# Rows of the down products' moving operand 64 bytes longer, in a gated encoder layer on one core

## The chip, the cores and the metric

The kernel runs on one core of a Trainium2 chip. A core has five engines that run side by side: TensorE (PE; its weight loads have a row of their own, PEld), VectorE (DVE), ScalarE (ACT), GpSimd (POOL) and SyncE (SP), which here only starts DMA transfers. Data for the engines lie in SBUF, a memory of 128 partitions; products of TensorE land in PSUM. The metric is the device time of one execution in microseconds (us). Before the change it is 1501.67 us, the median of three runs (1501.54 to 1502.61).

## The reference, cut to what matters

One layer of an encoder over 256 tokens with 2048 features, all in 32-bit floats. First come a normalization, an input projection, two kinds of attention with gates, and an output projection. Then, and this is the part that the change touches, a gated MLP with 5632 inner features:

```python
hf = rms_norm(x, ffn_norm[i])
g = dwconv_centred(hf @ w_ffn_gate[i], conv_w[i], conv_b[i])
x = x + (jax.nn.gelu(g) * (hf @ w_ffn_up[i])) @ w_ffn_down[i]
gate_p = jax.nn.sigmoid(rms_norm(x, ple_norm[i]) @ w_ple_gate[i])
x = x + gate_p * (p[i] @ w_ple_proj[i])
return rms_norm(x, final_norm)
```

The product with `w_ffn_down` is called the down product here.

## The kernel before, in words

Features lie on the partitions and tokens along the rows, so a product of a 128x128 weight block with 128 features of all 256 tokens is one step. To keep the precision of 32-bit floats on TensorE's float32r path, each operand is split into a high part and a remainder. A row of a moving operand (the one that streams through TensorE) holds the high parts of 256 tokens and then their remainders, 2T = 512 numbers or 2048 bytes.

*The weights.* All weights come as one stream of 128x128 blocks, in the order of use, by DMA from SyncE into `raw` (L174, three buffers of 16 blocks). For every eight blocks ACT makes the high parts `whi` (L190) and DVE the remainders `wlo` (L191), four buffers each. A block is 512 bytes of a partition.

*A step.* `block` (L195) multiplies the high block with the whole row (L201, 512 columns) and the remainder block with the row's first half (L202, 256 columns). Both add into a PSUM tile `acc`, of which three are used in turn. `product` (L207) runs the steps of one output block one after another; `wide_product` (L214) is the other way about, with weights streaming, for the attention values and the last two projections.

*The order.* `_plan` writes a list of jobs by hand, and the loop at L672 carries them out: the input projection with attention among it (`q`, `k`, `v`), gates and branch products (`ga`, `gb`, `ba`, `bb`), output projection (`o`), then twice, once for each half of the inner features: 22 gate (`g`) and 22 up (`u`) products of 16 steps each, and 16 down products (`d0`, `d1`) of 22 steps each. The small projection of the embedding (`pp`) and its gate (`pg`) come last. Work that follows a product is issued right behind it by `after` (L522) or at a step of a later job by `at`. Each engine works off its own instructions in the order of issue and waits on semaphores for the others.

*The moving operands.* `hs` (input projection and gates), `merged` (output projection) and `hf` (gate and up products) are tiles of the pool `big`, all named `mov` in the profile; `yab` holds the attention's results for the branch products. The down products read `act`, 22 rows, from the pool `ff`, allocated once for each half (L682) in one buffer. The last lines of `after` for an up product fill a row of it: `halves` copies the high part on ACT (L263) and subtracts on DVE (L264). Row k of `act` meets weight block k of the job.

*Places.* The allocator puts `act` at byte 154112 of each partition, behind it in the same pool `c`, `gw` (gate path), `pr`, `pw` (the embedding, `pw` split for the small projection), `ss`, `half`, `gate` and `sq4`. `mov` tiles are at 76960 and 109728, `whi` from 44192 and `wlo` from 60576.

Of the kernel before, what the change touches and what calls it, by code (L numbers as in the profile page):

```python
# [11 lines left out]
FR = mybir.dt.float32r  # L12
# [4 lines left out]
P = 128  # L17
T = 256
# [14 lines left out]
FHALF = FC // 2  # L33
# [100 lines left out]
def _encoder(ctx: ExitStack, tc, xt, pt, cols, table, onehot, mask, ident_in, last_gain, wts, out):  # L134
# [72 lines left out]
    def product(i, moving, n):  # L207
        acc = ps.tile([P, 2 * T], F32, name="acc", bufs=3)
        for k in range(n):
            run_due(i, k)  # L210
            block(acc, moving(k), k == 0, k == n - 1)
        return acc

    def wide_product(i, still, n, w, tag, places=HALVES, late=0):  # L214

        accs = [ps.tile([P, W4], F32, name="acc", tag=tag, bufs=3 if tag == "acc" else 2) for _ in places]

        def step(k, t, hi, lo):
            xh, xl = (still[:, k, c:c + T][:, places[t]] for c in (0, T))
            acc = accs[t][:, :w * P]
            nc.tensor.matmul(acc, xh, hi, start=(k == 0), stop=False)  # L224
            nc.tensor.matmul(acc, xh, lo, start=False, stop=False)  # L225
            nc.tensor.matmul(acc, xl, hi, start=False, stop=(k == n - 1))  # L226

        later = []
        for k in range(n):
            run_due(i, k)  # L230
            b = state["at"]
            s, o = _SUB_OF[b]
            split_to(s + 3)
            hi, lo = (m[:, o:o + w, :] for m in subs[s])
            step(k, 0, hi, lo)
            if k < n - late:
                step(k, 1, hi, lo)
            else:
                later.append((k, 1, hi, lo))
            state["at"] = b + w  # L240
            if o == _SUBS[s] - w:
                del subs[s]
        return accs, lambda: [step(*a) for a in later]
# [5 lines left out]
    def gather(acc, scale=1.0, u=None, keep=lambda ins: ins):  # L249

        t = sc.tile([P, T], F32, name="t")
        keep(nc.scalar.activation(t, acc[:, T:], AF.Copy, scale=scale))  # L252
        if u is None:
            u = sc.tile([P, T], F32, name="u")
        if scale == 1.0:
            nc.vector.tensor_tensor(u, acc[:, :T], t, op=ALU.add)  # L256
        else:
            nc.vector.scalar_tensor_tensor(u, acc[:, :T], scale, t, op0=ALU.mult, op1=ALU.add)
        return u

    def halves(dst, src):

        nc.scalar.activation(dst[:, :T], src, AF.Copy)  # L263
        nc.vector.tensor_tensor(dst[:, T:], src, dst[:, :T].bitcast(F32), op=ALU.subtract)  # L264
# [15 lines left out]
    def sums(totals, columns):  # L280

        s = ps.tile([P, len(columns)], F32, name="misc")
        for c, tokens in enumerate(columns):
            for i, total in enumerate(totals):
                nc.tensor.matmul(s[:, c:c + 1], total[:, tokens], ones[:, :1], start=(i == 0),
                                 stop=(i == len(totals) - 1))
        return s

    def root(s, n):

        v = sc.tile([P, n], F32, name="rv", bufs=3)
        nc.vector.tensor_scalar(v, s, 1.0 / D, EPS, op0=ALU.mult, op1=ALU.add)
        r = sc.tile([P, n], F32, name="rr", bufs=3)
        nc.gpsimd.tensor_tensor(r, v, mhalf[:, :n], op=ALU.pow)
        return r
# [15 lines left out]
    def rms(i, total, key, columns=HALVES):  # L311

        def ask():
            rc[key], dg = norm([total], columns)

            def tell():
                b = spread(dg)
                rt[key] = sc.tile([P, T], F32, name="rms")
                nc.scalar.activation(rt[key], b, AF.Copy)
            at(i[1], tell)  # L320
        at(i[0], ask)


    due, rt, rc, held = {}, {}, {}, {}

    def at(i, f, *a):

        due.setdefault(i, []).append((f, a))
# [343 lines left out]
    for i, job in enumerate(_JOBS):  # L672
        kind, n, _, _, _, blocks = job
        if kind == "ba" and n == 0:
            held["merged"] = big.tile([P, KC, 2 * T], FR, name="mov")
        if kind == "o" and n == 0:
            att.close()
            ff = held["ff"] = ctx.enter_context(tc.tile_pool(name="ff", bufs=1))
            held["hf"] = big.tile([P, KC, 2 * T], FR, name="mov")
            held["tot"] = sc.tile([P, T], F32, name="tot")  # L680
        if kind == "g" and n % FHALF == 0:
            held["act"] = ff.tile([P, FHALF, 2 * T], FR, name="act")  # L682
        if kind == "d1" and n == 0:
            held["pl"] = big.tile([P, KC, 2 * T], FR, name="mov")
            held["tot"] = sc.tile([P, T], F32, name="tot")
            pr = ff.tile([P, 2, T], F32, name="pr")
            nc.scalar.dma_start(pr, pt)
            pw = ff.tile([P, 2, 2 * T], FR, name="pw")
            for k in range(2):
                halves(pw[:, k, :], pr[:, k, :])  # L690
            held["ps"] = pw
            spare = big.tile([P, 2 * KC * T], F32, name="mov")
            held["rows"] = spare[:, :2 * D].rearrange("p (t n) -> p t n", t=2)
            held["lg"] = spare[:, 2 * D:3 * D]
            nc.scalar.dma_start(held["lg"], last_gain)
            held["ss"] = ff.tile([P, 2, QUARTERS], F32, name="ss")
        if kind == "g" and n == 0:
            rms([(i, 14), (i + 1, 9)], held["tot"], 1)
        if kind == "d1" and n % 2:
            at((i + 1, 9 if n < KC - 1 else 1), flip, n - 1)  # L700
        if kind == "pp" and n == 0:
            held["ph"] = ff.tile([P, 2, QUARTERS, W4], F32, name="ph", tag="act")
        if kind == "pp" and n == 2:
            half = held["half"] = held["ff"].tile([P, 2], F32, name="half")
            nc.vector.tensor_scalar(half, root(sums([held["tot"]], HALVES), 2), 0.5, None, op0=ALU.mult)
        if i < FIRST:
            firsts[i] = gather(firsts[i], SCALE if kind == "q" else 1.0,
                               ap_.tile([P, T], F32, name="first", tag="k", bufs=7), keep)
            continue
        if i == FIRST:  # L710
            rms([(START, 6), (START, 12)], tot, 0, HALVES + TWINS)
            for c, (h0, h) in enumerate([(0, 4), (4, 4), (8, 4), (12, 4), (16, 4)]):
                at(((FIRST, 8), (START + 1, 8), (START + 3, 8), (START + 5, 8), (START + 7, 8))[c], bias, h0, h)
        last = i == len(_JOBS) - 1
        rest = None
        if kind == "v":
            far = n[0] >= KVH + HG
            acc, _ = wide_product(i, hs, blocks, len(n), "sp" if far else "acc", TWINS if far else HALVES)
        elif kind in ("pp", "pg"):
            tag = "sp" if kind == "pp" else ("pt", "acc")[n % 2]  # L720
            acc, rest = wide_product(i, held["ps" if kind == "pp" else "pl"], blocks, 4, tag, late=4 if last else 0)
        else:
            acc = product(i, movers[kind], blocks)
        if i == FIRST:
            for e in range(FIRST):
                late = max(e - KVH, 0)
                at((START + late, 5 if late else 13), after, _JOBS[e], START, None, firsts[e])
            at((START, 13), after, job, START, acc)
        elif kind == "g" and n == 0:
            at((i + 1, 10), after, job, i, acc)  # L730
        elif kind == "pg":
            for t in range(2):
                if t:
                    rest()
                gate(n, t, acc[t], last)
                if last:
                    finish(t)
        else:
            after(job, i, acc)
# [48 lines left out]
```

## Time and profile before

| | |
|---|---|
| median of three runs | 1501.67 us (1501.54 to 1502.61) |
| profiled execution, whole | 1501.95 us |
| its span, first to last instruction | 1500.1 us |
| granted TensorE clock, mean | 0.998 |
| busy: PE, PEld | 1483.0 us, 1292.5 us |
| busy: DVE, ACT, POOL | 1045.0 us, 767.0 us, 4.6 us |
| DMA | 280.92 MB, 187 GB/s on average |
| down products, first half | 894.7 to 1018 us of the span |
| down products, second half | 1261.9 to 1388.6 us of the span |

A row of a group of instructions reads: line, engine, operation, output tile <- input tiles, shape, count, then busy time and mean duration, or least, median and largest duration with the first and the last start. Matmuls overlap: one is listed for longer than it keeps the next one waiting, since their ends are modelled. How fast TensorE goes through its steps is therefore read from starts, not from durations. "128*128 128x512" is a weight block of 128x128 with 512 columns streamed past it. Times within the span are counted from its start.

### The profile page before, as it was taken

How to read it: one execution, taken by the hardware profiler on the slowest of the kernel's cores; microseconds unless marked ns; L12 is line 12 of the kernel's file. 1: busy time of each engine (PE TensorE's matmuls, PEld its weight loads, DVE VectorE, ACT ScalarE, POOL GpSimd, SP SyncE). 2: the span in 40 equal slices, each digit the busy share in tenths (PEclk: the TensorE clock that was granted, in tenths of full speed). 3: DMA queues.
4: the chain of work that ended last, by engine and by line, in shares of the span. 5: the costliest groups of instructions: out<-in, count | busy, mean ns of one | idle time of the engine just before them, and what ended most of it. 6: DMA issues, size and time to landing. Idle time of an engine off the chain costs nothing.

```text
span 1500.1 us, 21525 instructions
## 1 busy us (share of the span) xinstructions
PE 1483.0 (99%) x8392; PEld 1292.5 (86%) x8392; DVE 1045.0 (70%) x1631; ACT 767.0 (51%) x1175; POOL 4.6 (0%) x9
## 2 busy tenths in 40 slices
PE   9999999999999999999999999999999999999996
PEld 8888888888888888888888888888888888888885
DVE  7685764666676776778888885557888887656564
ACT  7564544445555555555555554444555555555553
POOL 0000000000000000000000000000000000000000
PEclk9999999999999999999999999999999999999999
DMA  8744344445555555555555555554555555554552
GB/s 316 254 156 182 137 168 172 169 169 188 181 193 196 182 184 204 177 216 194 182 188 194 196 184 183 195 190 180 192 197 191 182 190 196 177 189 172 193 196 84
DMA packets 45233, 280.92 MB, mean 187 GB/s; under 512 B 4996, under 2 KB 9860, under 8 KB 12876
## 3 DMA queue, kind: packets, MB, share of 16 engines
q1 hardware_dynamic: 44268, 277.31, 51.7%
q10 hardware_dynamic: 864, 2.24, 0.4%
q8 instruction: 66, 1.08, 0.3%
q14 instruction: 35, 0.29, 0.1%
HBM read 277.39 MB, written 2.14 MB: 186 GB/s over the span
## 4 chain that ended last, share of the span: by engine, by line
PE 96%; DVE 2%; DMA 1%; ACT 1%; issue 0%; POOL 0%; SPq 0%; DVEq 0%; POOLq 0%; ACTq 0%
PE acc L201 53%; PE acc L202 27%; PE acc L224 4%; PE acc L226 4%; PE acc L225 4%; PE first L201 1%; PE first L202 1%; DVE wlo L191 1%; DMA raw<-in_wts 1%; PE pt L484 0%; PE misc L633 0%; DMA x<-in_xt 0%; PE misc L499 0%; PE sp L449 0%; ACT whi L190 0%
## 5 line engine op out<-in xcount | busy, mean ns | idle before, releaser
L191 DVE TENSOR_TENSOR wlo<-raw,whi 128x1024 fp32r<-128x1024 f32 (+1 forms) x519 | 632.0, 1218 | 407.4 <-ACT whi L190 407.1
L201 PE MATMUL acc<-mov,whi 128*128 128x512 f32 x2608 | 911.4, 394 | 1.5 <-DVE v L539 1.5
L190 ACT ACTIVATE whi<-raw 128x1024 fp32r<-128x1024 f32 (+1 forms) x519 | 547.6, 1055 | 645.0 <-PE acc L201 394.0
L202 PE MATMUL acc<-mov,wlo 128*128 128x256 f32 x2608 | 728.2, 279 | 0.0
L201 PEld LDWEIGHTS acc<-mov,whi 128*128 128x128 f32 x2608 | 488.6, 187 | 112.0 <-DVE v L539 1.7
L202 PEld LDWEIGHTS acc<-mov,wlo 128*128 128x128 f32 x2608 | 491.9, 189 | 0.2
L201 PE MATMUL acc<-act,whi 128*128 128x512 f32 x704 | 247.5, 394 | 0.0
L202 PE MATMUL acc<-act,wlo 128*128 128x256 f32 x704 | 196.5, 279 | 0.0
L201 PEld LDWEIGHTS acc<-act,whi 128*128 128x128 f32 x704 | 131.9, 187 | 31.1
L202 PEld LDWEIGHTS acc<-act,wlo 128*128 128x128 f32 x704 | 132.0, 187 | 0.0
L224 PE MATMUL acc<-whi,mov 128*128 128x512 f32 (+1 forms) x256 | 96.9, 379 | 0.0
L226 PE MATMUL acc<-whi,mov 128*128 128x512 f32 (+1 forms) x256 | 96.6, 377 | 0.0
L225 PE MATMUL acc<-wlo,mov 128*128 128x512 f32 (+1 forms) x256 | 96.6, 377 | 0.0
L252 ACT ACTIVATE t<-acc 128x256 f32<-128x256 f32 x227 | 83.1, 370 | 23.2 <-PE acc L202 23.2
L256 DVE TENSOR_TENSOR u<-acc,t 128x256 f32<-128x256 f32 x196 | 81.3, 418 | 2.4 <-ACT t L252 2.4
L201 PE MATMUL acc<-yab,whi 128*128 128x512 f32 x192 | 68.4, 395 | 0.0
L224 PEld LDWEIGHTS acc<-whi,mov 128*128 128x128 f32 x256 | 48.6, 190 | 9.3 <-DVE wlo L191 0.8
L226 PEld LDWEIGHTS acc<-whi,mov 128*128 128x128 f32 x256 | 48.6, 190 | 8.8
L225 PEld LDWEIGHTS acc<-wlo,mov 128*128 128x128 f32 x256 | 48.6, 190 | 8.6
L202 PE MATMUL acc<-yab,wlo 128*128 128x256 f32 x192 | 53.8, 280 | 0.0
L201 PEld LDWEIGHTS acc<-yab,whi 128*128 128x128 f32 x192 | 36.0, 188 | 8.8
L201 PE MATMUL first<-mov,whi 128*128 128x512 f32 x112 | 39.0, 400 | 0.8 <-DVE mov L269 0.8
(137 smaller groups left out, 856.5 us busy)
## 6 DMA issues: line engine op xcount, KB each, us to landing
raw<-in_wts SPq DMA_DIRECT2D x251, 1024.0 KB, 4.8
raw<-in_wts SPq DMA_DIRECT2D x12, 512.0 KB, 6.9
x<-in_xt SPq DMA_DIRECT2D x13, 128.0 KB, 6.0
mov<-hold SPq DMA_DIRECT2D x3, 514.0 KB, 6.4
mov<-hold SPq DMA_DIRECT2D x2, 768.0 KB, 7.1
mov<-in_last_gain ACTq DMA_DIRECT2D x1, 1024.0 KB, 4.8
out<-mov SPq DMA_DIRECT2D x2, 384.0 KB, 2.5
out<-mov ACTq DMA_DIRECT2D x2, 384.0 KB
```

What stands on the lines that cost most here:

```text
L190: nc.scalar.activation(hi, src, AF.Copy)
L191: nc.vector.tensor_tensor(lo, src, hi.bitcast(F32), op=ALU.subtract)
L201: nc.tensor.matmul(acc, hi[:, o, :], m, start=first, stop=False, skip_group_check=True)
L202: nc.tensor.matmul(acc[:, T:], lo[:, o, :], m[:, :T], start=False, stop=last, skip_group_check=True)
L224: nc.tensor.matmul(acc, xh, hi, start=(k == 0), stop=False)
L225: nc.tensor.matmul(acc, xh, lo, start=False, stop=False)
L226: nc.tensor.matmul(acc, xl, hi, start=False, stop=(k == n - 1))
L252: keep(nc.scalar.activation(t, acc[:, T:], AF.Copy, scale=scale))
L256: nc.vector.tensor_tensor(u, acc[:, :T], t, op=ALU.add)
```

## The change

Each row of `act` is allocated 16 numbers (64 bytes) longer, and the tile is cut back to its first 512 numbers per row at once, so that everything else reads and writes it as before:

```diff
         if kind == "g" and n % FHALF == 0:
-            held["act"] = ff.tile([P, FHALF, 2 * T], FR, name="act")
+            held["act"] = ff.tile([P, FHALF, 2 * T + 16], FR, name="act")[:, :, :2 * T]
```

Row k then starts at 154112 + 2112k bytes instead of 154112 + 2048k. The weight blocks stay where they are, 512 bytes apart, so the place of a row relative to its weight block, taken modulo 512 bytes, goes on by 64 bytes from each step to the next. The tiles behind `act` in the pool start 22 x 64 = 1408 bytes later.

## The prediction

> **What bounds the kernel now.** I read the page from the top (busy times, then the chain that ended last), then the busy times by stage, then the first and last start of the matmuls that read one operand, which give the spacing of a step.
>
> ```profile
> span 1500.1 us, 21525 instructions
> PE 1483.0 (99%) x8392; PEld 1292.5 (86%) x8392; DVE 1045.0 (70%) x1631; ACT 767.0 (51%) x1175; POOL 4.6 (0%) x9
> PE 96%; DVE 2%; DMA 1%; ACT 1%; issue 0%; POOL 0%; SPq 0%; DVEq 0%; POOLq 0%; ACTq 0%
> L201 PE MATMUL acc<-act,whi 128*128 128x512 f32 x704 | 247.5, 394 | 0.0
> L202 PE MATMUL acc<-act,wlo 128*128 128x256 f32 x704 | 196.5, 279 | 0.0
> ```
>
> TensorE is busy 99% of the span and carries 96% of the chain. The change touches the 704 pairs of matmuls that read `act`: 2 halves of 16 down products with 22 steps each, one L201 (512 columns) and one L202 (256 columns) per step. Neither line waited at all. By stage (stretch; length; busy time per engine; granted clock; DMA share; GB/s), the rows being the whole of the first half's down products, the second half's gate and up products, and the second half's down products:
>
> ```profile
> 894.50:1018.00 123.50, 123.50 (x707) 107.82 (x707) 67.74 (x80) 52.20 (x62) 0.00 (x0) 1.00 0.54 189
> 1018.00:1261.80 243.80, 243.80 (x1408) 214.94 (x1407) 198.65 (x349) 125.22 (x197) 0.00 (x0) 1.00 0.53 190
> 1261.80:1388.60 126.80, 126.80 (x734) 110.64 (x733) 78.37 (x109) 66.68 (x98) 0.00 (x0) 1.00 0.50 183
> ```
>
> In these stages PE is full at clock 1.00, while DVE works 67.74 of 123.50 us, ACT 52.20, and the DMA engines 54%. So the time here is the number of pairs times the spacing of a pair, and only a change of spacing can count.
>
> A matmul's listed duration (394 ns) overlaps the next one's and is no spacing. The spacing comes from the rows of a tile: first and last start, divided by the count less one. In order, for 512-column matmuls: `act` in the first half, `hf` (a tile named mov) in the second half's gate and up products, `merged` (also named mov) in the output projection, `yab` in the last branch products:
>
> ```profile
> L201 PE MATMUL acc<-act,whi x352: 392/394/397, 894.7 to 1017.5; 128*128 128x512 f32 x176
> ...
> L201 PE MATMUL acc<-mov,whi x673: 391/391/391, 1022.7 to 1255.7; 128*128 128x512 f32 x169
> ...
> L201 PE MATMUL acc<-mov,whi x206: 395/398/403, 571.2 to 643.6; 128*128 128x512 f32 x103
> ...
> L201 PE MATMUL acc<-yab,whi x25: 392/394/394, 550.3 to 558.7; 128*128 128x512 f32 x25
> ```
>
> Per pair: `act` 122.8 us / 351 = 349.9 ns; `hf` 233.0 / 672 = 346.7; `merged` 72.4 / 205 = 353.2; `yab` 8.4 / 24 = 350. The same two instructions with the same shapes take 346.7, 350 or 353.2 ns, at full clock and without a wait. So something of 3 ns per step, that the listed instructions don't show, does exist.
>
> **What could it be?** The built program gives the places in a partition of SBUF. All weight blocks start at 160 modulo 512 bytes (whi from 44192, wlo from 60576, 512 bytes per block). `hf` starts at 76960 and `merged` at 109728, both also 160 modulo 512, with rows of 2048 bytes; relative to the weights they are always at 0 modulo 512. `act` and `yab` start at 154112, which is 352 relative to the weights, at every step. So one relative place (352) has 350 ns in both its tiles, and the other (0) has both 346.7 and 353.2. So the relative place alone doesn't decide; how a stage is entered may. At the entry from the gate products (`hs`, another mov tile, at relative place 0) into one branch product, in order of time:
>
> ```profile
> 500.33 0.40 PE L201 MATMUL acc<-yab,whi 128*128 128x512 f32 x1
> 500.57 0.28 PE L202 MATMUL acc<-yab,wlo 128*128 128x256 f32 x1
> 500.69 0.39 PE L201 MATMUL acc<-yab,whi 128*128 128x512 f32 x1
> 500.92 0.28 PE L202 MATMUL acc<-yab,wlo 128*128 128x256 f32 x1
> 501.04 0.42 PE L201 MATMUL acc<-yab,whi 128*128 128x512 f32 x1
> 501.29 0.30 PE L202 MATMUL acc<-yab,wlo 128*128 128x256 f32 x1
> 501.43 0.39 PE L201 MATMUL acc<-yab,whi 128*128 128x512 f32 x1
> ...
> 501.77 0.40 PE L201 MATMUL acc<-yab,whi 128*128 128x512 f32 x1
> ...
> 502.13 0.39 PE L201 MATMUL acc<-yab,whi 128*128 128x512 f32 x1
> ...
> 502.48 0.39 PE L201 MATMUL acc<-yab,whi 128*128 128x512 f32 x1
> ```
>
> From 500.33 to 502.13 us are five pairs, 360 ns each, one of them 390 (501.04 to 501.43); after that the spacing is 350 again. A change of operand place can therefore cost five uneven steps, about 50 ns in all, before the pattern settles.
>
> **The change part by part.** (1) A row of `act` gets 64 bytes that nobody reads or writes. Instructions, their order on all five engines and the bytes moved by DMA stay as they are, so there is no term for added or removed work, and no queue is moved. (2) The place of row k relative to its weight block becomes 352 + 64k modulo 512, so eight steps go through 352, 416, 480, 32, 96, 160, 224, 288 and begin again, where it was 352 in every step. It never becomes 0. The price of a step at those seven new places is in no row. Bounds: below, the settled 346.7 ns of `hf`, that is 3.2 ns less per pair, 704 x 3.2 = 2.2 us less; above, every step as in the unsettled entry, 360 ns, 704 x 10 = 7.0 us more. I take 350, no change, for two reasons: it is what both tiles at an odd place have (350 and 349.9), and it is the middle between the two settled values on either side (346.7 and 353.2), which is what a round through many places averages to. Term: 0.0 us. (3) Writing `act`: 44 times an ACT copy and a DVE subtraction into a row that starts 64 bytes times k later.
>
> ```profile
> L263 ACT ACTIVATE act<-u x44: 399/404/411, 671.4 to 1265.9; 128x256 fp32r<-128x256 f32 x44
> L264 DVE TENSOR_TENSOR act<-u,act x44: 418/421/422, 672.8 to 1267.1; 128x256 fp32r<-128x256 f32 x44
> ```
>
> The rows stay contiguous, and the spread of the 44 is 12 and 4 ns, so 44 x 16 ns = 0.7 us at most, under PE's work (DVE has 45 us of 243.8 free in the gate and up stage). If that cover were gone it would be those 0.7 us. Term: 0. (4) `act` grows by 22 x 64 = 1408 bytes, and the tiles behind it in its pool (`c`, `gw`, `pr`, `pw`, `ss`, `half`, `gate`, `sq4`) start 1408 bytes later. Only `pw` is read by TensorE, as the stationary operand of the 48 matmuls of the small projection, whose durations differ from those with a mov tile by at most 11 ns:
>
> ```profile
> L226 PE MATMUL acc<-whi,pw x3: 395/398/400, 1399.9 to 1401.3; 128*128 128x512 f32 x3
> ...
> L224 PE MATMUL acc<-whi,mov x118: 389/389/389, 1403.8 to 1483.3; 128*128 128x512 f32 x118
> ```
>
> So 48 x 11 ns = 0.5 us either way; I take 0, its place being as odd after as before. (5) The 28 transposes between the second half's down products stay where they are:
>
> ```profile
> L633 PE MATMUL misc<-ident,x x28: 270/272/332, 1280.5 to 1376.3; 128*128 128x128 f32 x28
> ```
>
> They read neither `act` nor a moved tile. Term: 0.
>
> The sum is 0.0 us. The profiled execution took 1501.95 us, 1500.1 of span and 1.85 around it; it is 0.28 above the median of the three runs, 1501.67. On the median the forecast is 1501.7 us.
>
> **Against the Trainium skill.** The rows show spacings that differ by 3.2 ns with the place of the moving operand. The Trainium skill, "TensorE: Matmul & The Clock Gate", section "Step-by-step: what each phase is for", says that TensorE has two independent SBUF read ports, one for the streamed operand and one for LDWEIGHTS, so that a weight load takes no read bandwidth from the running matmul. By that rule the relative place cannot matter and the change would be worth exactly 0, and every rival below falls. The trace agrees only in part, since 346.7, 350 and 353.2 ns stand beside each other, so the rivals keep their chances.
>
> **The rivals.** A measurement of this kernel (1501.54 to 1502.61 in three runs) can tell about 0.2%, 3.0 us, from no change; spread over 704 pairs that is 4.3 ns each.
>
> *Fast settling:* the walk through the places ends the pattern of `act` and the pairs run at 346.7. For it: two stages at 346.7 (the row of `hf`). Against: at 352 no pair row has it. 1501.7 - 2.2 = 1499.5 us, still within 0.2%.
>
> *Below the best spacing:* at some places the hidden delay goes altogether. The shortest spacings are those of the first half's gate and up products:
>
> ```profile
> 672.45 0.39 PE L201 MATMUL acc<-mov,whi 128*128 128x512 f32 x1
> 672.68 0.27 PE L202 MATMUL acc<-mov,wlo 128*128 128x256 f32 x1
> 672.79 0.40 PE L201 MATMUL acc<-mov,whi 128*128 128x512 f32 x1
> 673.02 0.28 PE L202 MATMUL acc<-mov,wlo 128*128 128x256 f32 x1
> 673.14 0.39 PE L201 MATMUL acc<-mov,whi 128*128 128x512 f32 x1
> ```
>
> One pair takes 340 ns (672.45 to 672.79), but the next 350. If all had 340 it would be 704 x 10 = 7.0 us less, 1494.7. Against it: every short pair is paid back by the next one.
>
> *Never settled, the rival on the slower side:* each step changes the relative place, as an entry does, so the pattern of five uneven steps never ends. Full price 704 x 10 ns = 7.0 us, 1508.7; it decides from 4.3 ns per pair on, when the mean passes 354.3. For it: the entry rows above. Against: that entry jumps by 352 bytes and not by 64, and in the steady stages the weights' block also moves by 512 bytes in each step without unsettling anything.
>
> *A later stage settles badly:* the down products are left in another pattern than now, and the second half's gate and up products (704 pairs, no stall in between to change the pattern) run like the output projection, 353.2 instead of 346.7: 704 x 6.5 = 4.6 us, 1506.3. For it: both values occur at the same relative place. Against: the same products are entered now from `act` at 349.9, and settled at 346.7.
>
> *It does nothing at all:* what matters repeats within 64 bytes, or isn't SBUF. Then the pairs stay at 349.9 and the time at 1501.7; this can't be told from the likeliest by the time, only by unchanged spacings at every step.
>
> **How the numbers follow.** No change of mean spacing, whether by averaging or because nothing depends on it: 0.62. Fast settling: 0.12. Below the best: 0.04. Never settled: 0.11. A later stage badly settled: 0.11. Faster by over 0.2% is the third, with a little of the second: 0.05. Slower is the last two: 0.22. Same: 0.73. The range goes down to fast settling with the 0.2 us of run noise, 1499.3, and up to the badly settled later stage, 1506.5; it leaves out the third and the upper part of the fourth, about 0.1. The likeliest one's own range is 1500.7 to 1502.7, the 0.5 us of `pw` and as much of noise.
>
> **What would show it.** The count and spread of `act` rows as above: 349.9 ns per pair if right, 346.7 or over 354 in the rivals; a pattern over eight steps in place of the present even one would show that place matters at all. The spacing of `hf` in the second half (346.7) would show a badly settled later stage. The forecast is wrong if a place among the seven costs tens of ns, like the single step of 390 above: two such steps in eight would be 704 x 10 = 7.0 us.

## The result

The changed kernel takes 1507.61 us (median of five runs, 1506.93 to 1509.28) against 1501.71 (1501.54 to 1502.99); the ratio is 1.0038, with a 95% interval of 1.0025 to 1.0051. It is slower by some 5.9 us, more than the forecast's range (1499.3 to 1506.5) allows, and no run of one kernel lies among those of the other.

The page of the changed kernel, span, busy times and chain:

```profile
span 1506.8 us, 21525 instructions
PE 1490.1 (99%) x8392; PEld 1294.5 (86%) x8392; DVE 1045.4 (69%) x1631; ACT 767.2 (51%) x1175; POOL 4.7 (0%) x9
PE 97%; DVE 2%; ACT 1%; DMA 0%; issue 0%; POOL 0%; DVEq 0%; POOLq 0%; ACTq 0%
```

The same instructions, the same bound, and TensorE busy for 7.1 us more. By stage (first half's down products, second half's gate and up products, second half's down products; columns as before):

```profile
894.50:1019.30 124.80, 124.80 (x711) 108.48 (x710) 68.76 (x81) 52.44 (x62) 0.00 (x0) 1.00 0.51 189
1019.30:1268.00 248.70, 248.70 (x1410) 215.69 (x1409) 198.96 (x349) 125.20 (x197) 0.00 (x0) 1.00 0.51 186
1268.00:1395.20 127.20, 127.20 (x734) 110.79 (x733) 78.39 (x109) 66.68 (x98) 0.00 (x0) 1.00 0.50 183
```

PE is full and its clock 1.00 in all three, as before. The middle stage, whose code and operands the change doesn't touch, grew from 243.8 to 248.7 us by the ends of these stretches. The rows of the 512-column matmuls, in the order of the three stages:

```profile
L201 PE MATMUL acc<-act,whi x352: 389/396/398, 895.7 to 1019.2; 128*128 128x512 f32 x176
...
L201 PE MATMUL acc<-mov,whi x661: 395/398/403, 1024.8 to 1258.0; 128*128 128x512 f32 x166
...
L201 PE MATMUL acc<-act,whi x351: 388/396/481, 1268.2 to 1394.7; 128*128 128x512 f32 x176
```

A pair of the first half's down products takes 123.5 us / 351 = 351.9 ns where it took 349.9. A pair of the second half's gate and up products takes 233.2 / 660 = 353.3 where it took 346.7: 704 x 6.6 ns = 4.6 us. From the first start of `act` to its first start in the second half it is 1268.2 - 895.7 = 372.5 us against 367.2, 5.3 us more; from there to the end of the span 238.6 against 238.2, 0.4 more. (Another 1.0 us of this profile lies ahead of the first down product, in a part that the change doesn't reach; starts there differ by as much between runs.) So 4.6 of some 5.7 us came in a stage behind the changed one. The slow spacing there is not even: L201 starts at 1019.84, 1020.19, 1020.55, 1020.90, 1021.25 and 1021.61 us, so every third pair takes 360 ns and the others 350. Before, every pair of this stage took 346 or 347 ns once the first was over.

The pattern inside a down product is uneven now. The L201 starts of one product's first steps, in order of time:

```profile
911.14 0.40 PE L201 MATMUL acc<-act,whi 128*128 128x512 f32 x1
...
911.49 0.39 PE L201 MATMUL acc<-act,whi 128*128 128x512 f32 x1
...
911.84 0.40 PE L201 MATMUL acc<-act,whi 128*128 128x512 f32 x1
...
912.20 0.39 PE L201 MATMUL acc<-act,whi 128*128 128x512 f32 x1
...
912.54 0.40 PE L201 MATMUL acc<-act,whi 128*128 128x512 f32 x1
...
912.90 0.39 PE L201 MATMUL acc<-act,whi 128*128 128x512 f32 x1
```

Their spacings are 350, 350, 360, 340 and 360 ns, and the other products of this half repeat the sequence to within 2 ns. From the eighth step on the spacings lie between 349 and 355 ns and repeat every four steps. In the kernel before they are 349 and 351 in turn, so the place of the row does matter.

### The profile page after: what moved, and what is told of

Read it like the earlier page. It is cut to its first block, busy times and chain, and to the rows that moved or that the text cites. A ratio compares the mean times of both kernels' runs of the same rounds, so it can differ in the third digit from the quotient of the medians.

```text
span 1506.8 us, 21525 instructions
## 1 busy us (share of the span) xinstructions
PE 1490.1 (99%) x8392; PEld 1294.5 (86%) x8392; DVE 1045.4 (69%) x1631; ACT 767.2 (51%) x1175; POOL 4.7 (0%) x9
## 4 chain that ended last, share of the span: by engine, by line
PE 97%; DVE 2%; ACT 1%; DMA 0%; issue 0%; POOL 0%; DVEq 0%; POOLq 0%; ACTq 0%
PE acc L201 53%; PE acc L202 27%; PE acc L224 4%; PE acc L225 4%; PE acc L226 4%; PE first L201 2%; PE first L202 1%; PE pt L484 0%; DVE wlo L191 0%; PE misc L633 0%; DMA x<-in_xt 0%; PE misc L499 0%; PE sp L449 0%; PE misc L430 0%; PE misc L431 0%
## 5 line engine op out<-in xcount | busy, mean ns | idle before, releaser
L201 PE MATMUL acc<-mov,whi 128*128 128x512 f32 x2608 | 916.3, 396 | 1.5 <-DVE v L539 1.5
L201 PEld LDWEIGHTS acc<-mov,whi 128*128 128x128 f32 x2608 | 489.2, 188 | 116.4 <-DVE v L539 1.7
L201 PE MATMUL acc<-act,whi 128*128 128x512 f32 x704 | 248.7, 396 | 0.0
L201 PEld LDWEIGHTS acc<-act,whi 128*128 128x128 f32 x704 | 132.0, 187 | 32.0
L201 PE MATMUL acc<-yab,whi 128*128 128x512 f32 x192 | 68.4, 395 | 0.0
L201 PEld LDWEIGHTS acc<-yab,whi 128*128 128x128 f32 x192 | 36.0, 188 | 8.8
L201 PE MATMUL first<-mov,whi 128*128 128x512 f32 x112 | 40.3, 410 | 0.8 <-DVE mov L269 0.8
```

Of the source, the lines that this page charges most:

```text
L201: nc.tensor.matmul(acc, hi[:, o, :], m, start=first, stop=False, skip_group_check=True)
```

## The experiments

I went in with an *entry theory*: the slow gate and up products (353.3 ns) take over a timing from the down products ahead of them. Against it stood a *pool theory*: the 1408 bytes by which the small tiles behind `act` moved are what slows them. In the kernels with their own rows for `act`, the three places where it is made and used read

```diff
-            held["act"] = ff.tile([P, FHALF, 2 * T], FR, name="act")
+            flat = ff.tile([P, FHALF * (2 * T + 16)], FR, name="act")
+            held["act"] = [flat[:, o:o + 2 * T] for o in STARTS]
-            halves(held["act"][:, n % FHALF, :], u)
+            halves(held["act"][n % FHALF], u)
-        "d": lambda k: held["act"][:, k, :],
+        "d": lambda k: held["act"][k],
```

and only STARTS differs, in numbers of 4 bytes. The flat tile is as long as in the changed kernel, unless said otherwise. Ratios are to the kernel before, run beside, with 95% intervals.

**Which half.** STARTS is `[k * (2 * T + 16 * (n == 0)) for k in range(FHALF)]`.

> Rows 64 bytes longer in the first half's down products alone; the second half's are at 2048 bytes again, in a tile of the longer size. Entry theory (the second half's gate and up products take over a slow pattern from the down products ahead of them): down products of the first half 351.8 ns per pair as in the changed kernel, gate and up products of the second half 353.3, second half's down products back at 350.0; in all 0.64 + 4.66 us, about 1507.0. Pool theory (the tiles behind act, moved by 1408 bytes, slow the second half's gate and up products): the same 353.3, so this run alone doesn't part the two; it does against a third one, that the padded rows act only where they are read, which gives 346.7 and 1502.3.

Measured: 1508.13 us, ratio 1.0038 (1.0025 to 1.0051). The first half brings the loss; the 0.4 us of the second half, which this kernel lacks, is less than the times can tell. The gate and up products of the second half:

```profile
L201 PE MATMUL acc<-mov,whi x661: 395/398/403, 1024.7 to 1257.9; 128*128 128x512 f32 x166
```

233.2 / 660 = 353.3 ns. The second half alone, `16 * (n > 0)`:

> Rows 64 bytes longer in the second half's down products alone. Entry theory: first half's down products 350.0 ns per pair, second half's gate and up products 346.7, second half's down products some 1.4 ns more than before per pair, in all 0.4 us more, about 1502.1. Pool theory: the small tiles are moved as in the changed kernel, so the second half's gate and up products stay at 353.3, about 1506.8.

Measured: 1502.32 us, ratio 1.0003 (0.9994 to 1.0013). The gate and up products of the second half stayed as before:

```profile
L201 PE MATMUL acc<-mov,whi x670: 391/391/391, 1023.8 to 1255.7; 128*128 128x512 f32 x168
```

(1255.7 - 1023.8) / 669 = 346.6 ns. The small tiles are moved here too, so the pool theory falls.

**The moved tiles alone.** STARTS is `[k * 2 * T for k in range(FHALF)]`.

> Rows at 2048 bytes in both halves, but the tile as long as in the changed kernel, so that only the tiles behind it (c, gw, pr, pw, ss, half, gate, sq4) move by 1408 bytes. Entry theory: every stage as before, 1501.7. Pool theory: second half's gate and up products at 353.3 ns per pair, 1506.3.

Measured: 1501.76 us, ratio 1.0001 (0.9992 to 1.0010), with both stages as before:

```profile
L201 PE MATMUL acc<-act,whi x352: 392/394/397, 894.1 to 1016.9; 128*128 128x512 f32 x176
...
L201 PE MATMUL acc<-mov,whi x670: 391/391/391, 1023.9 to 1255.8; 128*128 128x512 f32 x168
```

**One row.** STARTS is `[k * 2 * T + (336 if k == FHALF - 1 else 0) for k in range(FHALF)]`.

> Rows at 2048 bytes but for the last one of each half (row 21), which lies where the changed kernel has it, at 160 modulo 512 bytes relative to its weight block; one step in 22. If the place of the last step before the gate and up products decides their pattern: 353.3 ns per pair in the second half's gate and up products, and about 1506.3 us. If what decides is the timing that the walk through all the places leaves: 346.7 and about 1501.8. Down products: 350.0 in either case but for the two steps at each change of place, some 0.1 us in all.

Measured: 1507.11 us, ratio 1.0035 (1.0022 to 1.0047).

```profile
L201 PE MATMUL acc<-act,whi x352: 392/393/397, 894.7 to 1017.6; 128*128 128x512 f32 x176
...
L201 PE MATMUL acc<-mov,whi x660: 395/398/403, 1024.9 to 1257.7; 128*128 128x512 f32 x165
```

The down products run at 122.9 / 351 = 350.1, as before, but 232.8 / 659 = 353.3 ns follow. One row of 22, in one step per product, costs nothing that shows in its own stage and sets the 704 pairs behind it to the slow spacing. The reverse, the walk with only its last row put back (`[k * (2 * T + 16) + (48 if k == FHALF - 1 else 0) for k in range(FHALF)]`, the tile 192 bytes longer):

> Rows 64 bytes longer as in the changed kernel, but the last row of each half set back to the relative place that it had before (352 modulo 512 bytes). If the last step's place decides the pattern of the products behind it: gate and up products of the second half at 346.7 ns per pair although the walk stays, down products at 351.8, in all some 1.1 us more than before, about 1502.8. If the walk itself leaves a timing that ends in the slow pattern: 353.3 ns and about 1507.5.

Measured: 1502.47 us, ratio 1.0005 (0.9996 to 1.0014).

```profile
L201 PE MATMUL acc<-act,whi x352: 389/396/398, 894.4 to 1017.8; 128*128 128x512 f32 x176
...
L201 PE MATMUL acc<-mov,whi x671: 391/391/391, 1023.7 to 1256.0; 128*128 128x512 f32 x168
```

The walk costs 123.4 / 351 = 351.6 ns per pair in the down products, and 346.7 follow. So the two parts of the loss come apart: the walk, and the entry.

**Other places for the last row.** The 336 of the one-row kernel becomes 16, then 104.

> Only the last row of each half displaced, by 64 bytes, to 416 modulo 512 relative to its weight block. The place 352 led into the fast pattern and 160 into the slow one. If slow entries come with many places: 353.3 in the second half's gate and up products, 1506.4. If 160 is one unlucky place of few: 346.7, 1501.8. I take the second to be as likely as the first; the run tells how much of a lottery the change was.

> Only the last row of each half displaced, by 416 bytes, to 256 modulo 512 relative to its weight block; a third place for the same question. Slow entry: 353.3 and 1506.4; fast entry: 346.7 and 1501.8.

Measured: 1507.22 us at 416 modulo 512 (ratio 1.0032, 1.0019 to 1.0046) and 1503.16 at 256 (1.0002, 0.9991 to 1.0012). The first row is of the former, the second of the latter:

```profile
L201 PE MATMUL acc<-mov,whi x661: 395/398/403, 1024.7 to 1257.9; 128*128 128x512 f32 x166
```

```profile
L201 PE MATMUL acc<-mov,whi x673: 391/391/391, 1025.9 to 1258.8; 128*128 128x512 f32 x169
```

Of four last places, 352 and 256 lead into 346.7 ns, and 160 and 416 into 353.3.

**Is it the relative place?** Everything moves by 32 bytes:

```diff
+    const.tile([P, 8], F32, name="filler")
     x = const.tile([P, KC, T], F32, name="x")
```

> The kernel before with an unused tile of 32 bytes ahead of all others but the small constants, so that every operand of the products, weights and moving rows alike, lies 32 bytes later, and their places relative to each other stay. If only the relative place counts: down products at 350.0, second half's gate and up products at 346.7, output projection at 353.2, all as before, 1501.7. If the moving row's own place counts, modulo 64 bytes or finer: act would lie like mov does now and the other way about, and the spacings change places: down products at 346.7 or 353.3, gate and up products at 350.0 (1408 pairs x 3.3 ns = 4.6 us more, less 2.3 us), about 1504.

Measured: 1502.49 us, ratio 1.0002 (0.9992 to 1.0012). The down products (lines are one further here), the gate and up products of the second half and the output projection:

```profile
L202 PE MATMUL acc<-act,whi x352: 392/394/397, 894.2 to 1017.0; 128*128 128x512 f32 x176
...
L202 PE MATMUL acc<-mov,whi x671: 391/391/391, 1023.6 to 1255.9; 128*128 128x512 f32 x168
...
L202 PE MATMUL acc<-mov,whi x205: 395/398/403, 570.7 to 642.8; 128*128 128x512 f32 x103
```

That is 349.9, 346.7 and 353.4 ns, all as before. A shift that all operands in SBUF share changes nothing, at least not one of 32 bytes. So this run speaks for the relative place, without settling it: a place of the moving row alone, counted in units well above 32 bytes, would fit as well, and neither a larger shift nor the weights moved without the rows was tried.

**Place zero.** STARTS is `[40 + k * 2 * T for k in range(FHALF)]`.

> Rows at 2048 bytes, but all of act begins 160 bytes later, so that every row of it lies at 0 modulo 512 bytes relative to its weight block, as hf and merged do (the tiles behind it as in the changed kernel). If place decides which patterns there are: the down products run at one of the two spacings of that place, 346.7 (704 x 3.3 ns = 2.3 us less, 1499.4) or 353.3 (1504.0), and not at 350; coming from gate and up products in the fast pattern at the same place, the fast one is likelier in the first half. If place is not what makes 350: 350.0 and 1501.7.

Measured: 1501.65 us, ratio 1.0000 (0.9990 to 1.0009). The first half's down products, and the second and the fourth of the second half (each row with one step of the product ahead):

```profile
L201 PE MATMUL acc<-act,whi x352: 392/394/395, 893.8 to 1015.5; 128*128 128x512 f32 x176
...
L201 PE MATMUL acc<-act,whi x23: 392/392/395, 1267.1 to 1274.8; 128*128 128x512 f32 x23
...
L201 PE MATMUL acc<-act,whi x23: 395/398/403, 1282.9 to 1290.7; 128*128 128x512 f32 x23
```

The first half runs at 121.7 / 351 = 346.7. The two rows of single products are too short for that, since their times are rounded to 0.1 us (7.7 / 22 is 350 for one, 7.8 / 22 is 355 for the other); there the listed durations tell the fast pattern (392) and the slow one (395 to 403) apart. Behind the first transposes the slow one came and stayed. The second half's down products whole, before and with place zero:

```profile
L201 PE MATMUL acc<-act,whi x352: 389/394/481, 1261.9 to 1388.3; 128*128 128x512 f32 x176
```

```profile
L201 PE MATMUL acc<-act,whi x352: 392/398/478, 1259.8 to 1386.8; 128*128 128x512 f32 x176
```

From first to last start it is 127.0 us against 126.4: the second half gave back 0.6 of the 1.1 us that the first had won, and the rest is less than the times can tell. At 352 the same transposes left the products between them at 350.0 ns. Place zero in the first half alone (`(40 if n == 0 else 0) + k * 2 * T`):

> The kernel before with act 160 bytes later in the first half's down products alone (0 modulo 512 relative to the weights, where they ran at 346.7 ns per pair when both halves were moved), the second half's at its old place, where the transposes between its products did no harm. If places can be chosen stage by stage: 346.7, 346.7 and 350.0 in the three stages, 352 x 3.3 ns = 1.2 us less than before, 1500.5 beside 1501.7. If the second half's gate and up products or its down products settle badly for it: up to 4.6 us more.

Measured: 1500.59 us against 1501.86, ratio 0.9994 (0.9985 to 1.0003).

```profile
L201 PE MATMUL acc<-act,whi x352: 392/394/395, 894.9 to 1016.6; 128*128 128x512 f32 x176
...
L201 PE MATMUL acc<-mov,whi x670: 392/394/395, 1022.8 to 1254.8; 128*128 128x512 f32 x168
```

121.7 us instead of 122.8, and the stage behind it at 346.8: the expected 1.2 us stand in the trace, while the interval of the times still includes no change.

**Can the slow pattern be left?** One transpose more (a jolt, in what follows) in the changed kernel, and the same in the kernel before, in its output projection (kind `o`, n 2):

```diff
+        if kind == "g" and n == FHALF + 1:
+
+            def jolt():
+                p = ps.tile([P, P], F32, name="misc")
+                nc.tensor.transpose(p, ident, ident)
+            at((i, 0), jolt)
```

> The changed kernel with one 128x128 transpose more on TensorE (of the identity, into a PSUM tile that nobody reads), ahead of the second gate product of the second half. If the slow spacing is a pattern that only lasts because nothing disturbs it, one matmul of another length may throw it into the fast one: 346.7 ns from there on, 4.4 us less than the changed kernel plus 0.1 for the transpose, about 1503.2. If the spacing is set by the places of the operands alone, or the jolt leads back into the same pattern: 353.3 and about 1507.7.

> The kernel before with one 128x128 transpose more on TensorE ahead of the third product of the output projection, whose pairs run at 353.2 ns in a pattern that begins behind a late row in its first product. If the jolt throws it into the fast pattern: 346.7 ns in the 14 products left, 224 x 6.6 ns = 1.5 us less, 1500.3. If not: 353.2 and 1501.8.

Measured: 1507.29 us (ratio 1.0036, 1.0023 to 1.0049), and 1502.12 (1.0001, 0.9992 to 1.0011). The row of the former's gate and up products: 230.0 / 651 = 353.3 ns. In the latter, the output projection behind the jolt has 67.9 / 192 = 353.6. First the former's row, then the latter's:

```profile
L201 PE MATMUL acc<-mov,whi x652: 395/398/403, 1031.8 to 1261.8; 128*128 128x512 f32 x163
```

```profile
L201 PE MATMUL acc<-mov,whi x193: 395/398/403, 575.3 to 643.2; 128*128 128x512 f32 x193
```

Then several sizes in one kernel, `for _ in range(count)` around the transpose, ahead of six up products of the second half:

> The changed kernel with jolts of six sizes in the second half's up products: 2, 3, 4, 5, 6 and 8 transposes of the identity (into a PSUM tile that nobody reads) ahead of up products 2, 5, 8, 11, 14 and 17 of that half. One transpose left the slow pattern as it was. If a longer jolt leads out of it, one of these stretches and all behind it run at 346.7 ns per pair until a later jolt throws it back, and the time is up to 4 us less than the changed kernel. If the slow pattern withstands whatever only shifts it in time: 353.3 in all stretches, and 28 transposes of some 84 ns, 2.4 us, more than the changed kernel, about 1510.

Measured: 1509.55 us (ratio 1.0046, 1.0030 to 1.0062). Ahead of the last jolt and behind it (lines are one further here):

```profile
L202 PE MATMUL acc<-mov,whi x64: 395/398/403, 1195.6 to 1217.9; 128*128 128x512 f32 x64
```

```profile
L202 PE MATMUL acc<-mov,whi x114: 391/391/475, 1224.7 to 1263.9; 128*128 128x512 f32 x114
```

2 to 6 transposes left the slow pattern as it was: the first row, from behind the 6, has 22.3 / 63 = 354 ns. After the 8 ahead of up product 17 it is 39.2 / 113 = 346.9. Eight transposes alone, ahead of the second gate product of the changed kernel:

> The changed kernel with 8 transposes of the identity more ahead of the second gate product of the second half, where one alone changed nothing. If 8 transposes lead out of the slow pattern whenever they come: 346.7 ns from there on, 688 x 6.6 = 4.5 us less for 0.7 us of transposes, about 1503.8 against the changed kernel's 1507.6. If it depends on the moment: 353.3, and 1508.3.

Measured: 1504.37 us against 1501.86, ratio 1.0015 (1.0006 to 1.0024): 2.5 us above the kernel before, where the changed kernel was 5.9 above it. The gate and up products behind it, and the down products ahead of it, with the walk as in the changed kernel:

```profile
L201 PE MATMUL acc<-mov,whi x669: 391/391/396, 1024.3 to 1255.8; 128*128 128x512 f32 x168
...
L201 PE MATMUL acc<-act,whi x352: 389/396/398, 893.5 to 1017.0; 128*128 128x512 f32 x176
```

231.5 / 668 = 346.6 ns, and 351.9 ahead of it. So the stage behind the walk is slow for the timing that it starts with, and for nothing in its operands. Whether the number of transposes counts or the moment at which they come is not shown: 2 to 6 were tried once each, 1 and 8 at more than one moment, 7 not at all. Last, the 8 transposes in the output projection, with place zero in the first half:

> The same with 8 transposes of the identity more ahead of the third output product. If 8 transposes lead out of the slow pattern whenever they come: 13 or 14 products of 16 pairs at 346.7 instead of 353.2, 1.4 us less, for 0.7 us of transposes; 1499.8. If it depends on the moment at which they come: 353.2 may stay there and the time is 0.7 us above the kernel without them.

Measured: 1511.38 us, ratio 1.0066 (1.0053 to 1.0079), the slowest of all and 11.6 us above what was expected. Rows of the output projection, the first half's gate and up products, its down products, and the second half's gate and up products:

```profile
L201 PE MATMUL acc<-mov,whi x205: 391/391/391, 578.0 to 648.7; 128*128 128x512 f32 x103
...
L201 PE MATMUL acc<-mov,whi x638: 395/398/403, 667.8 to 892.9; 128*128 128x512 f32 x160
...
L201 PE MATMUL acc<-act,whi x352: 395/398/403, 899.6 to 1023.6; 128*128 128x512 f32 x176
...
L201 PE MATMUL acc<-mov,whi x669: 395/398/403, 1029.6 to 1265.7; 128*128 128x512 f32 x168
```

The jolt did what was expected of it: 70.7 / 204 = 346.6 ns in the output projection. But the first half's gate and up products now run at 225.1 / 637 = 353.4. Between the two patterns lie the small matmuls of the normalization (L285 where the first gate product ends, L308 in the second); in both traces the listed durations change right behind L285. In the kernel before, the slow pattern ahead of them (353.2) became the fast one behind them, 216.4 / 624 = 346.8 ns:

```profile
L201 PE MATMUL acc<-mov,whi x625: 392/392/395, 672.4 to 888.8; 128*128 128x512 f32 x157
```

Here the fast one became the slow one, and it lasted through down products at place zero (124.0 / 351 = 353.3) to the second half's end of up products (236.1 / 668 = 353.4), 1760 pairs.

## Why the prediction was wrong

**What bounds the kernel** held: PE full, clock 1.00, no waits, and the time is pairs times spacing. **Reading spacings from starts** was what found the cause; busy shares show it only as 99%.

**Part (2), the walk through the places,** was taken as 0.0 us, as an average of what lies on either side. It measured 351.9 ns against 349.9 in the first half (123.5 us against 122.8) and 0.4 us in the second, 1.1 us in all. That is inside its bounds (2.2 less to 7.0 more) and mis-sized by 1.1 us.

**The step that failed** is that the sum stopped at the 704 pairs whose operands change and put nothing for the pairs behind them. The second half's gate and up products carry 4.6 us of the loss. This was the rival *a later stage settles badly*, with its price, 4.6 us and 1506.3, right; with the walk's 1.1 us it makes 1507.4. It was given 0.11 on the argument that the same products are entered from `act` and settle at 346.7. They were entered from the last row's old place. The one-row kernel (353.3 behind the new place) and its reverse (346.7 behind the old one, with the walk) show that the last row's place decides here. With two of four tried places leading into the slow pattern, few as four are, an even chance would have been the better figure, and range and forecast would have moved up.

**Never settled** was right that the steps stay uneven and wrong in its price: their mean is 351.9 ns, not 360. The 360 was the mean of the five pairs at one entry into a branch product; the entry into `act` itself, in the kernel before, has one step of 354 ns and then 349 and 351 in turn. **Fast settling** was wrong for this walk. Down products at 346.7 were seen only at place zero and entered from the fast pattern, in two kernels; in the third one with place zero they were entered from the slow pattern and ran at 353.3. **It does nothing at all** is ruled out by the one-row kernel.

**Part (3),** writing `act`, at 0: right; the median copy took 402 ns and the median subtraction 419 in the changed kernel, 404 and 421 before. **Part (4),** the moved tiles, at 0: right, by the kernel with only the moved tiles (1501.76, both stages as before). **Part (5),** the transposes: right at place 352, and wrong as a rule, since at place zero they threw the pattern from fast to slow.

**The page of the Trainium skill** ("TensorE: Matmul & The Clock Gate", section "Step-by-step: what each phase is for") holds that a weight load takes no read bandwidth from a running matmul. No run here measured that bandwidth. That the place of a moving row is therefore free was the prediction's inference, and the runs contradict it: 346.7, 350 and 353.3 ns, and 1507.11 against 1501.71 us for one moved row. What in TensorE or SBUF makes the place count was not tried. That the streams of weights and moving rows get into each other's way is the likely reading of the shift by 32 bytes that changed nothing, but it is argued and not shown.

## What to carry to other kernels

Where one engine is full for a whole stage, read its step from first and last start, stage by stage, and compare stages with the same instructions: a spacing that differs without a wait can be, as here, a pattern that the stage has fallen into, and a change upstream can flip it. A padding of an operand is then priced by the pairs that read it and by every pair that comes after it undisturbed. Before padding, move one row alone; and an alignment that wins in one stage may only do so because nothing disturbs it there.

## What was not expected of the hardware

A pair of a 512-column and a 256-column matmul runs at 346.7, 350.0 or 353.3 ns at full clock; the three lie 3.3 ns apart. At place zero there are two patterns, 346.7 and 353.3, and TensorE kept the one it had, across tiles and stages, until something disturbed it: the slow one for 1760 pairs in the last experiment's kernel. In products with all rows at 352 modulo 512 only 350.0 was seen once they had settled, also behind the slow pattern (in the second half of the kernel with longer rows in the first half alone). Up to 6 transposes did not end the slow pattern, 8 did in all three kernels that had them, and the same small matmuls of the normalization turned slow into fast in one kernel and fast into slow in another. What decides between the two when a stage begins was not found, beyond the last step's place.
